# A transformer block whose MLP runs as seven block products: another order of the products, two pairs of them chained in PSUM, half-size load slots, and a rearranged end

## The chip, the core and the metric

The kernel runs on one core of one Trainium2 chip, the other cores being idle. The metric is device microseconds (us) for one execution. The kernel before takes 2223.9 us in the median of three runs (2223.78 to 2226.18).

## The reference, cut to what matters

One block: attention and retention branches, an output projection, a residual, then the MLP. All is float32, 512 tokens, model width 2048, MLP width 8192. The change touches nothing ahead of the MLP's residual, so the rest is shown alone:

```python
    x = x + rms_norm(mix, norm_mix_post[l])
    h = rms_norm(x, norm_mlp_pre[l])
    u = jnp.square(jax.nn.relu(h @ w_up[l]))            # [512, 2048] @ [2048, 8192]
    x = x + rms_norm(u @ w_down[l], norm_mlp_post[l])   # [512, 8192] @ [8192, 2048]
```

## The kernel before, in words

**Seven products.** Each of the two matrix products of the MLP is cut into 2 x 2 parts and computed with seven products P0 to P6 instead of eight, after Strassen and Winograd. Each product multiplies a sum of parts of the activations with a sum of parts of the weights: P0 takes weight part 11, P1 takes 21, P5 takes 22, P2 takes 11+12, P3 takes 12+22, P4 takes 11+12+22 and P6 all four (the tables `ADD` and `SPLIT`). Sums of the products' results give the output: P0+P1 is output part 11, and so on.

**Three matmuls for one.** Float32 is kept by splitting every operand into a high part (fp32r) and the rest: `hi = cast(x)` on ScalarE, `lo = x - hi` on VectorE. `mm3` issues hi by hi, hi by lo and lo by hi into one PSUM tile.

**The up stage** goes through 16 blocks of 2 x 256 columns of w_up; a product is 48 matmuls of 256 columns. **The down stage** goes through 8 chunks of w_down's rows times 2 halves (nb) of its columns, with seven products each; a product is 24 matmuls of 512 columns, and its result is added to one of 14 accumulators in SBUF by VectorE (L1365).

**Order.** A list of phases (block, product) is written out by hand. At its head stand nine early phases, products 0 and 1 of blocks 0 to 3 and product 0 of block 4, which run while the residual, the norm and the sums of the activations (`work3`: `x1_chain`, `x1_out`, `x1_sums`) are still being made. Then come blocks 0, 4, 1, 5, 2, 6, 3, 7, 8 to 15. Blocks 0 to 3 are short there, since two of their products are done.

**The feed.** `Feed` brings the weights: quarters of 1 MB go into slots (`low0`, `low1`, two rows of `Y`, and three lent ones at first) by SyncE's DMA queue (L925). Each product is fed in two slabs of 128 x 1024: where the weight is a sum, VectorE adds it into the slot (L951); ScalarE casts the high part (`whi`, L956); VectorE subtracts (`wlo`, L931) one slab later. The feed stays three slabs ahead of TensorE. For P3 the second summand comes by an accumulating DMA on GpSimd's queue (`late_sum`, L917), but not in blocks 0 to 3. A slot is free again when both its slabs are split.

**Other work.** `up_done` combines the products of a block (VectorE and ScalarE) and stores seven operands of the down stage to DRAM (`keep_u`, L1126, SyncE's queue). `u_operand` loads and splits them for the next chunk (L1288 to L1290). `dn_done` accumulates; in the last chunk it also combines the accumulators (L1370), squares them for the norm (ScalarE, L1310), multiplies by the gain (L1315), takes the roots (L1329, L160, GpSimd L161) and writes the result: rows 0 and 1 of the four token tiles scaled by ScalarE and added into DRAM by accumulating DMAs (`out_first`, L1340, L1341), rows 2 and 3 by VectorE and plain DMAs (`out_last`, L1348, L1349).

Of the kernel before, what the change touches and what calls it, by code (L numbers as in the profile page):

```python
# [10 lines left out]
F32 = mybir.dt.float32  # L11
# [101 lines left out]
def block_kernel(ctx: ExitStack, tc: tile.TileContext, x, norm_mix_pre, w_in, cmp_pe_k, cmp_w1_k, cmp_b1_k,  # L113
# [39 lines left out]
    def mm3(ps, ah, al, bh, bl, first, last):  # L153
        nc.tensor.matmul(ps, ah, bh, start=first, stop=False)  # L154
        nc.tensor.matmul(ps, ah, bl, start=False, stop=False)  # L155
        nc.tensor.matmul(ps, al, bh, start=False, stop=last)  # L156
# [706 lines left out]

    ADD = (None, None, (11, 12), (12, 22), (11, 22), None, (11, 21))
# [20 lines left out]

    class Feed:
# [5 lines left out]
        def __init__(self, phases, slots, ahead, short):  # L892
            self.phases, self.free, self.ahead, self.lent = phases, list(slots), ahead, []
            self.short = short
            self.n, self.at, self.R, self.ready = 0, 0, {}, {}
            self.loads, self.last = [], {}
            for i, (g, prod, source) in enumerate(phases):
                for q in (SPLIT[prod],) if self.by_dma(i) else (ADD[prod] or ()) + (SPLIT[prod],):
                    if (g, q) not in self.last:
                        self.loads.append((g, q, source, i))  # L900
                    self.last[g, q] = i
            self.held = None

        def by_dma(self, i):

            g, prod, _ = self.phases[i]
            return prod == 3 and g not in self.short

        def late_sum(self, i):
# [4 lines left out]
            k = src.shape[1]  # L914
            r = self.R[g, to].rearrange("p (k n) -> p k n", k=k)
            for h in (slice(0, k // 2), slice(k // 2, k)):
                nc.gpsimd.dma_start(r[:, h], src[:, h], accum_op=ALU.add)  # L917

        def load(self, most=99):
            while most and self.loads and self.free and self.loads[0][3] <= self.n // 2 + self.ahead:  # L920
                most -= 1
                g, q, source, _ = self.loads.pop(0)
                r = self.R[g, q] = self.free.pop(0)
                src = source(q)
                nc.sync.dma_start(r.rearrange("p (k n) -> p k n", k=src.shape[1]), src)  # L925

        def low(self):
# [6 lines left out]
            if s:  # L934
                for q in (11, 12, 21, 22):
                    if self.last.get((self.phases[i][0], q)) == i:
                        r = self.R.pop((self.phases[i][0], q))
                        if all(r is not o for o in self.lent):
                            self.free.append(r)

        def advance(self):
# [6 lines left out]
            c = slice(s * SL, (s + 1) * SL)  # L948
            if ADD[prod] and not self.by_dma(i):
                to, by = (self.R[g, q][:, c] for q in ADD[prod])  # L950
                nc.vector.tensor_add(to, to, by)  # L951
            src = self.R[g, SPLIT[prod]][:, c]
# [7 lines left out]
            if prod == 2 and s and (j := [j for j in range(i, min(i + 5, len(self.phases))) if self.by_dma(j)]):  # L960
                self.late_sum(j[0])
# [55 lines left out]
    def x1_out(t):  # L1017
# [16 lines left out]
        for q in range(4):  # L1034
# [5 lines left out]
            nc.vector.tensor_tensor(Y4[:, ks, t, :], pt4, g3T[:, ks, None].to_broadcast([P, 4, P]), op=ALU.mult)  # L1040
# [63 lines left out]
    phases += [(b, p, up_source(b)) for b in blocks for p in ((5, 2, 4, 3, 6) if 0 < b < NPRO else ORDER)  # L1104
# [12 lines left out]
    feed = Feed(phases, [low0, low1], 3, range(NPRO))  # L1117
    tmp = Ring(*xt, *(xh[:, c:c + 512] for c in range(0, 2048, 512)))
    state = [{} for _ in range(NBLK)]

# [4 lines left out]
    def keep_u(k, b, v):  # L1125
        nc.sync.dma_start(ud[k, b], v)  # L1126

    def up_done(b, p, ps):
# [12 lines left out]
        elif p == 1:  # L1141
            z["c11"] = tmp.take()
            nc.vector.tensor_add(v2(z["c11"]), ps, v2(z["p0"]))
            hidden(0, z["c11"])
        elif p == 2:
            if b == 0:
                tmp.views = [Y[:, t, c:c + 512] for t in (1, 3) for c in range(0, 2048, 512)]
            elif b == NPRO:
                tmp.views += xt[:2]
            elif b == NPRO + 1:  # L1150
                tmp.views += xt[2:]
# [336 lines left out]
```

## Time and profile before

| | us |
|---|---|
| median of three runs | 2223.9 |
| the profiled execution | 2220.96 |
| its span, first to last instruction | 2219.2 |
| TensorE busy | 2161.8 (97%) |
| VectorE busy | 1575.4 (71%) |
| ScalarE busy | 994.2 (45%) |
| the MLP's early phases | from about 939 |
| the up stage's full blocks without a gap on TensorE | 1216 to 1570 |
| the down stage up to the last chunk | about 1575 to 2110 |
| the last matmul ends | about 2200.7 |

TensorE is busy nearly all the time, so what it does not do in the remaining 57 us, and how long it is given half its clock, is where time can be found. Busy time is read with care: a matmul's record is longer than the step from one matmul to the next, so a stretch is best measured by how many matmuls it holds.

### The profile page before, as it was taken

What the parts mean: (1) busy time and instruction counts of PE and PEld (TensorE: products, weight loads), DVE (VectorE), ACT (ScalarE), POOL (GpSimd) and SP (SyncE); (2) the same over time, 40 slices, a digit from 0 to 9 for tenths busy, and PEclk for the clock granted to TensorE, in tenths of its full rate; (3) what the DMA queues carried; (4) which work ended last, traced back from release to release, by engine and by line L of the source; (5) the groups of instructions that cost most, each with busy time, mean ns of one, the idle gap of its engine ahead of it and who ended that gap; (6) DMA issues with size and microseconds to landing.
All of it is one profiled execution on the core that took longest, in us unless ns stands there. A gap on an engine that the chain in (4) does not pass through costs nothing.

```text
span 2219.2 us, 31801 instructions
## 1 busy us (share of the span) xinstructions
PE 2161.8 (97%) x12787; PEld 1915.4 (86%) x12787; DVE 1575.4 (71%) x1880; ACT 994.2 (45%) x1440; POOL 111.1 (5%) x131
## 2 busy tenths in 40 slices
PE   8999999999999999989999999999999999999995
PEld 7888878878778899989999999999888888888874
DVE  6213555554556533598888878878879999999998
ACT  5213343343332323575555555555664454445443
POOL 0000000000000000000000000000000000000001
PEclk9999999999999999999999999999999999999998
DMA  6543324323224334565655766767675656566664
GB/s 192 136 122 88 93 65 95 95 72 91 81 72 138 98 103 142 186 221 171 207 172 169 225 179 183 190 174 209 223 229 161 216 163 218 160 197 175 192 187 86
DMA packets 248054, 342.67 MB, mean 154 GB/s; under 512 B 14011, under 2 KB 159755, under 8 KB 247009
## 3 DMA queue, kind: packets, MB, share of 16 engines
q1 hardware_dynamic: 213440, 292.43, 40.6%
q0 software_dynamic: 24368, 36.67, 10.3%
q10 hardware_dynamic: 10098, 11.55, 1.5%
q8 instruction: 100, 1.64, 0.3%
q14 instruction: 48, 0.39, 0.1%
HBM read 298.85 MB, written 41.75 MB: 153 GB/s over the span
## 4 chain that ended last, share of the span: by engine, by line
PE 87%; DVE 8%; ACT 2%; issue 1%; DMA 1%; POOL 0%; SPq 0%; DVEq 0%; POOLq 0%; ACTq 0%
PE prod L156 16%; PE prod L155 16%; PE prod L154 16%; PE mm L154 11%; PE mm L156 11%; PE mm L155 11%; DVE wlo L931 2%; PE S L583 2%; PE S L706 1%; PE PT L646 1%; PE oT L741 1%; PE oT L501 1%; PE oT L154 1%; DVE Y L951 1%; DMA low<-in_w_up 1%
## 5 line engine op out<-in xcount | busy, mean ns | idle before, releaser
L956 ACT CAST whi<-low 128x1024 fp32r<-128x1024 f32 x230 | 242.1, 1053 | 277.5 <-PE prod L156 134.9
L155 PE MATMUL prod<-wlo,Hh 128*128 128x512 f32 x896 | 350.5, 391 | 11.5 <-DVE wlo L931 11.4
L956 ACT CAST whi<-Y 128x1024 fp32r<-128x1024 f32 x212 | 222.6, 1050 | 285.7 <-PE prod L156 119.9
L144 DVE TENSOR_TENSOR wlo<-raw,whi 128x1024 fp32r<-128x1024 f32 (+4 forms) x152 | 168.6, 1113 | 255.4 <-ACT whi L143 250.6
L156 PE MATMUL prod<-whi,Hl 128*128 128x512 f32 x896 | 349.4, 390 | 0.0
L154 PE MATMUL prod<-whi,Hh 128*128 128x512 f32 x896 | 349.3, 390 | 0.0
L931 DVE TENSOR_TENSOR wlo<-low,whi 128x1024 fp32r<-128x1024 f32 x230 | 280.1, 1221 | 48.2 <-ACT whi L956 47.3
L156 PE MATMUL prod<-Hh,wlo 128*128 128x256 f32 x1024 | 285.3, 279 | 13.4 <-DVE wlo L931 13.4
L931 DVE TENSOR_TENSOR wlo<-Y,whi 128x1024 fp32r<-128x1024 f32 x212 | 258.4, 1221 | 38.7 <-ACT whi L956 37.7
L154 PE MATMUL prod<-Hh,whi 128*128 128x256 f32 x1024 | 284.7, 278 | 0.3 <-ACT Hh L143 0.3
L155 PE MATMUL prod<-Hl,whi 128*128 128x256 f32 x1024 | 284.0, 277 | 0.9 <-DVE Hl L144 0.9
L143 ACT CAST whi<-raw 128x1024 fp32r<-128x1024 f32 (+4 forms) x152 | 145.6, 960 | 302.2 <-PE mm L155 148.0
L154 PE MATMUL mm<-whi,Hh 128*128 128x416 f32 (+4 forms) x704 | 263.1, 374 | 0.5 <-ACT Hh L143 0.5
L156 PE MATMUL mm<-whi,Hl 128*128 128x416 f32 (+4 forms) x704 | 248.6, 353 | 0.5 <-DVE Hl L144 0.5
L155 PE MATMUL mm<-wlo,Hh 128*128 128x416 f32 (+4 forms) x704 | 248.1, 352 | 0.0
L156 PE MATMUL prod<-sx,wlo 128*128 128x256 f32 x768 | 212.3, 276 | 2.6 <-DVE wlo L931 2.6
L154 PE MATMUL mm<-Hh,whi 128*128 128x512 f32 x512 | 214.7, 419 | 0.1
L154 PE MATMUL prod<-sx,whi 128*128 128x256 f32 x768 | 212.0, 276 | 0.0
L155 PE MATMUL prod<-sx,whi 128*128 128x256 f32 x768 | 212.0, 276 | 0.0
L155 PEld LDWEIGHTS prod<-wlo,Hh 128*128 128x128 f32 x896 | 168.7, 188 | 49.7 <-DVE wlo L931 14.8
L156 PEld LDWEIGHTS prod<-Hh,wlo 128*128 128x128 f32 x1024 | 192.9, 188 | 15.3 <-DVE wlo L931 15.2
L156 PE MATMUL mm<-Hh,wlo 128*128 128x512 f32 x512 | 200.5, 392 | 0.0
(265 smaller groups left out, 3969.9 us busy)
## 6 DMA issues: line engine op xcount, KB each, us to landing
raw<-in_w_in SPq DMA_DIRECT2D x160, 256.0 KB, 3.1
low<-in_w_up SPq DMA_DIRECT2D x38, 1024.0 KB, 6.0
Y<-in_w_up SPq DMA_DIRECT2D x32, 1024.0 KB, 6.3
Y<-in_w_down SPq DMA_DIRECT2D x32, 1024.0 KB, 5.2
low<-in_w_down SPq DMA_DIRECT2D x32, 1024.0 KB, 5.2
Y<-ud SPq DMA_DIRECT2D x49, 512.0 KB, 9.0
ud<-Y SPq DMA_DIRECT2D x77, 256.0 KB, 4.3
raw<-in_w_out SPq DMA_DIRECT2D x32, 416.0 KB, 3.5
```

Of the source, the lines that this page charges most:

```text
L143: nc.scalar.copy(hi, src)
L144: nc.vector.tensor_sub(lo, src, hi.bitcast(F32))
L154: nc.tensor.matmul(ps, ah, bh, start=first, stop=False)
L155: nc.tensor.matmul(ps, ah, bl, start=False, stop=False)
L156: nc.tensor.matmul(ps, al, bh, start=False, stop=last)
L501: nc.tensor.matmul(hid[:65, :DK], kv[:, l:l + STRIDE * 64 + 1:STRIDE], w1s[l // 16][:, l % 16, :], start=l == 0, stop=l == CBLK - 1)
L583: nc.tensor.matmul(sps[:, :c + L], QT[g][:, h, qs], k, start=True, stop=True)
L646: nc.tensor.transpose(pt[:, e * P:(e + 1) * P], Pt[:, e, rows_of(j)], ident)
L706: nc.tensor.matmul(sps[:, :n], QK[:, 2 + d, rows_of(j)], QK[:, d, j * P:], start=d == 0, stop=d == 1)
L741: nc.tensor.matmul(o[:, :DR], AT[:, a0:a0 + P], vr[:, j, :], start=j == 0, stop=j == i)
L931: nc.vector.tensor_sub(lo, src, hi.bitcast(F32))
L956: nc.scalar.copy(hi, src)
```

## The change

- **Order of the products.** A full block and every down group run 0 2 1 4 3 5 6 (before 0 1 2 5 4 3 6). Blocks 0 to 4 run 1 2 5 4 3 6 less what the early phases did. The early phases go through two blocks together: P0 of both, then P1 of both.
- **Chains in PSUM.** P1 accumulates onto P0's PSUM tile, with P2 between them; in the down groups and from block 5 on, P6 accumulates onto P3's, with P5 between. A class `Banks` hands out the three PSUM tile pairs. P0 and P3 are still read out when they are done.
- **Sums in `up_done`** are rearranged to fit: P0+P1 comes out of PSUM through ScalarE's Relu (before: an add on VectorE, then Relu), P3 is subtracted straight from PSUM.
- **Half slots.** Loads, slots and releases are by halves of 512 KB, in the order in which slabs need them; there are six lent halves.
- **P3's second summand by DMA everywhere**, and in the last chunk P6's as well (`tight`).
- **`keep_u`** issues from ScalarE's queue (before SyncE's).
- **x1_out**: for token tiles 2 and 3 half of the gains are applied by ScalarE, four instructions of 128 x 128, in place of one of VectorE.
- **The last chunk**: accumulators of one row lie side by side, so that the output is scaled and written 1024 columns at a time; the roots of rows 0 and 1 stay after the last P5, but scaling and writing these rows move behind the last product's first half.

```diff
-        def __init__(self, phases, slots, ahead, short):
+        def __init__(self, phases, slots, ahead, tight):
+            self.phases, self.free, self.ahead, self.lent = phases, [h for r in slots for h in halved(r)], ahead, []
...
-            return prod == 3 and g not in self.short
+            return prod == 3 or prod == 6 and g in self.tight
...
-            if s:
-                for q in (11, 12, 21, 22):
-                    if self.last.get((self.phases[i][0], q)) == i:
-                        r = self.R.pop((self.phases[i][0], q))
+            for q in (11, 12, 21, 22):
+                if self.last.get((self.phases[i][0], q)) == i:
+                    r = self.R.pop((self.phases[i][0], q, s))
...
+            if t >= 2 and q % 2:
+                for j in range(4):
+                    k = 4 * q + j
+                    nc.scalar.activation(Y4[:, k, t, :], pt4[:, j, :], AF.Copy, scale=g3T[:, k:k + 1])
+            else:
+                nc.vector.tensor_tensor(Y4[:, ks, t, :], pt4, g3T[:, ks, None].to_broadcast([P, 4, P]), op=ALU.mult)
...
-    ORDER = (0, 1, 2, 5, 4, 3, 6)
-    early = [(b, p) for b in range(NPRO) for p in (0, 1)] + [(NPRO, 0)]
+    ORDER = (0, 2, 1, 4, 3, 5, 6)
+    early = [(b + n, p) for b in range(0, NPRO, 2) for p in (0, 1) for n in (0, 1)] + [(NPRO, 0)]
...
+    class Banks:
+
+
+        def __init__(self):
+            self.free, self.held = [pr0], {}
+
+        def chained(self, g, p):
+
+            b = g if isinstance(g, int) else g[0]
+            return p in (0, 1) and b != NPRO or p in (3, 6) and (b == "down" or b > NPRO)
+
+        def take(self, g, p):
+
+            group = g if not isinstance(g, int) and g[0] == "down" else g if isinstance(g, int) else g[0]
+            if self.chained(g, p) and p in (1, 6):
+                self.now = self.held.pop((group, p))
+                self.free.append(self.now[0])
+                return self.now[1], True
+            pool = self.free.pop(0)
+            ps = pool.tile([P, 2, S], F32, name="prod")
+            if self.chained(g, p):
+                self.held[group, {0: 1, 3: 6}[p]] = pool, ps
+            else:
+                self.free.append(pool)
+            return ps, False
...
     def keep_u(k, b, v):
-        nc.sync.dma_start(ud[k, b], v)
+        nc.scalar.dma_start(ud[k, b], v)
...
+                nc.scalar.activation(v2(z["c11"]), ps, AF.Relu)
+                later.add(1, lambda: nc.scalar.activation(z["c11"], z["c11"], AF.Square))
+                later.add(3, lambda: keep_u(0, b, z["c11"]))
...
+            z["c22"] = tmp.take()
+            nc.vector.tensor_sub(v2(z["c22"]), v2(z["v"]), ps)
+            hidden(6, z["c22"])
...
+        else:
+            lasts = []
+            for t in (0, 1):
+                add(e[6][:, t], ps[:, t], e[6][:, t])
+                square(1, 21, 2 + t, e[6][:, t])
+                gained(1, 21, e[6], slice(t, t + 1))
+                for parts in lasts:
+                    next(parts)
+                root(2 + t)
+                out_first(t)
+                lasts.append(out_last(2 + t))
+                next(lasts[-1])
+            next(lasts[-1])
```

What this does to VectorE at the beginning of short block 1, before, from P2's second `wlo` on (`low` and `Y` are weight slots; a row on 128x1024 with two slots is a weight sum, the 128x512 rows combine products):

```order
L1184 TENSOR_TENSOR Y_5587<-Y_5587 128x512
L951 TENSOR_TENSOR Y_5587<-Y_5587,low1_7097 128x1024
L931 TENSOR_TENSOR wlo_8862<-Y_5587,whi_8861 128x1024
L951 TENSOR_TENSOR Y_5587<-Y_5587,low1_7097 128x1024
L931 TENSOR_TENSOR wlo_8897<-Y_5587,whi_8896 128x1024
L951 TENSOR_TENSOR low0_7099<-low0_7099,low1_7097 128x1024
L931 TENSOR_TENSOR wlo_8931<-Y_5587,whi_8930 128x1024
L951 TENSOR_TENSOR low0_7099<-low0_7099,low1_7097 128x1024
L931 TENSOR_TENSOR wlo_8961<-low0_7099,whi_8960 128x1024
```

and now, from P5's second `wlo` on, through P4 and P3 to P6's first sum:

```order
L1232 TENSOR_TENSOR Y_5587<-Y_5587 128x512
L956 TENSOR_TENSOR Y_5587<-Y_5587 128x1024
L938 TENSOR_TENSOR wlo_8894<-Y_5587,whi_8893 128x1024
L956 TENSOR_TENSOR Y_5587<-Y_5587 128x1024
L938 TENSOR_TENSOR wlo_8928<-Y_5587,whi_8927 128x1024
L938 TENSOR_TENSOR wlo_8962<-Y_5587,whi_8961 128x1024
L938 TENSOR_TENSOR wlo_8992<-low1_7097,whi_8991 128x1024
L956 TENSOR_TENSOR Y_5587<-Y_5587,low0_7099 128x1024
```

P3's two weight sums have left VectorE, and P4's stand between products that need none.

VectorE's last rows before the final product, before (`acc` and `xh` are accumulators, `xrow` the gain; the last two `wlo` feed the final product):

```order
L1370 TENSOR_TENSOR acc9_14666<-acc9_14666,acc7_14664 128x1024
L951 TENSOR_TENSOR low0_7099<-low0_7099,low1_7097 128x1024
L931 TENSOR_TENSOR wlo_18788<-Y_5587,whi_18787 128x1024
L1365 TENSOR_TENSOR acc11_14668<-prod_18764,acc11_14668 128x1024
L1370 TENSOR_TENSOR xh_7103<-xh_7103,acc9_14666 128x1024
L1370 TENSOR_TENSOR xh_7103<-xh_7103,acc7_14664 128x1024
L1315 TENSOR_TENSOR acc8_14665<-acc8_14665,xrow_7098 128x1024
L1389 TENSOR_TENSOR xh_7103<-xh_7103,acc11_14668 128x1024
L1370 TENSOR_TENSOR acc9_14666<-acc9_14666,acc11_14668 128x1024
L951 TENSOR_TENSOR low0_7099<-low0_7099,low1_7097 128x1024
L931 TENSOR_TENSOR wlo_18807<-low0_7099,whi_18806 128x1024
L931 TENSOR_TENSOR wlo_18834<-low0_7099,whi_18833 128x1024
```

and now (`two` and `xh` hold two accumulators each):

```order
L1431 TENSOR_TENSOR acc10_14679<-prod_18769,acc10_14679 128x1024
L1419 TENSOR_TENSOR two2_14675<-two2_14675,acc10_14679 128x1024
L938 TENSOR_TENSOR wlo_18812<-low1_7097,whi_18811 128x1024
L1419 TENSOR_TENSOR xh_7103<-xh_7103,two2_14675 128x1024
L938 TENSOR_TENSOR wlo_18830<-Y_5587,whi_18829 128x1024
L1419 TENSOR_TENSOR two2_14675<-two2_14675,acc13_14680 128x1024
L1439 TENSOR_TENSOR two2_14675<-two2_14675,prod_18810 128x1024
L1419 TENSOR_TENSOR two2_14675<-two2_14675,acc10_14679 128x1024
L938 TENSOR_TENSOR wlo_18848<-Y_5587,whi_18847 128x1024
L938 TENSOR_TENSOR wlo_18871<-Y_5587,whi_18870 128x1024
```

The two weight sums of the final product are gone from here. From the read-out of the last chunk's first P0 to the last `wlo`, both included, VectorE had 69 rows and has 59.

GpSimd's last rows before (`st` 5588 to 5591 are the statistics of rows 0 to 3, the DMAs add rows 0 and 1 into the output):

```order
L161 TENSOR_TENSOR st_5588<-st_5588,misc 128x1
L161 TENSOR_TENSOR st_5589<-st_5589,misc 128x1
L1341 DMA out<-acc_14658 128x512
L1341 DMA out<-acc_14662 128x512
L1341 DMA out<-acc_14665 128x512
L1341 DMA out<-xh 128x512
L1341 DMA out<-acc_14658 128x512
L1341 DMA out<-acc_14662 128x512
L1341 DMA out<-acc_14665 128x512
L1341 DMA out<-xh 128x512
L161 TENSOR_TENSOR st_5590<-st_5590,misc 128x1
L161 TENSOR_TENSOR st_5591<-st_5591,misc 128x1
```

and now:

```order
L162 TENSOR_TENSOR st_5588<-st_5588,misc 128x1
L162 TENSOR_TENSOR st_5589<-st_5589,misc 128x1
L162 TENSOR_TENSOR st_5590<-st_5590,misc 128x1
L1393 DMA out<-two_14673 128x2x512
L1393 DMA out<-xh 128x2x512
L162 TENSOR_TENSOR st_5591<-st_5591,misc 128x1
L1393 DMA out<-two_14673 128x2x512
L1393 DMA out<-xh 128x2x512
```

The accumulating output DMAs now stand behind the roots of rows 2 and 3.

## Rows read from the trace of the kernel before

**Rows 1.** The page's busy time: us, share of the span, instructions.
```profile
PE 2161.8 (97%) x12787; PEld 1915.4 (86%) x12787; DVE 1575.4 (71%) x1880; ACT 994.2 (45%) x1440; POOL 111.1 (5%) x131
```
**Rows 2.** Windows: stretch, length, busy us (instructions) of PE PEld DVE ACT POOL, PEclk, DMA.
```profile
939.00:1000.00 61.00, 55.08 (x460) 54.30 (x460) 54.70 (x63) 41.88 (x56) 2.68 (x3) 0.97 0.69 229
1000.00:1216.00 216.00, 205.69 (x1788) 204.01 (x1787) 180.13 (x183) 112.75 (x139) 7.68 (x6) 1.00 0.61 183
1216.00:1570.00 354.00, 354.00 (x3120) 354.00 (x3119) 290.12 (x292) 197.76 (x242) 22.92 (x18) 1.00 0.68 190
1600.00:2100.00 500.00, 500.00 (x2207) 414.17 (x2206) 450.81 (x390) 245.25 (x240) 30.75 (x26) 1.00 0.62 187
2100.00:2200.80 100.80, 89.69 (x377) 71.41 (x376) 100.00 (x92) 46.94 (x66) 9.16 (x12) 0.97 0.46 133
```
**Rows 3.** PE's waits in 939:1000, 1000:1216, 2090:2220: us in total, times, longest.
```profile
PE prod L156 <- DVE wlo L931: 5.8, 4, 3.8
...
PE prod L156 <- DVE wlo L931: 10.3, 8, 1.9
...
PE prod L155 <- DVE wlo L931: 11.0, 6, 6.0
```
**Rows 4.** Timeline of DVE in short block 1: start, us, instruction [idle before <-releaser].
```profile
1064.52 1.23 DVE L951 TENSOR_TENSOR Y<-Y,low 128x1024 f32<-128x1024 f32 x1 [2.55 <-DMA low<-in_w_up]
...
1072.32 1.22 DVE L951 TENSOR_TENSOR Y<-Y,low 128x1024 f32<-128x1024 f32 x1
1073.46 1.22 DVE L931 TENSOR_TENSOR wlo<-Y,whi 128x1024 fp32r<-128x1024 f32 x1
```
**Rows 5.** Timeline of ACT, then of DVE, near the end of the early phases.
```profile
977.81 1.05 ACT L956 CAST whi<-low 128x1024 fp32r<-128x1024 f32 x1 [2.36 <-DMA low<-in_w_up]
...
981.45 1.23 DVE L144 TENSOR_TENSOR Hl<-Y,Hh 128x1024 fp32r<-128x1024 f32 x1 [1.71 <-ACT Hh L143]
...
995.08 1.21 DVE L931 TENSOR_TENSOR wlo<-low,whi 128x1024 fp32r<-128x1024 f32 x1
```
**Rows 6.** DVE's groups in 1216:1570 by shape: count, busy us, mean ns.
```profile
L931 DVE TENSOR_TENSOR wlo<-low,whi 128x1024 fp32r<-128x1024 f32 x68 | 82.7, 1223 | 20.8 <-ACT whi L956 20.4
...
L1163 DVE TENSOR_TENSOR Y<-Y 128x512 f32<-128x512 f32 x7 | 4.8, 692 | 0.2
```
**Rows 7.** DVE's timeline in the last chunk: first P0 read out; last two `wlo`.
```profile
2114.99 1.22 DVE L1365 TENSOR_TENSOR acc<-prod,acc 128x1024 f32<-128x1024 f32 x1
...
2191.78 2.47 DVE L931 TENSOR_TENSOR wlo<-low,whi 128x1024 fp32r<-128x1024 f32 x2
```
**Rows 8.** Timeline of the end.
```profile
2197.42 2.69 POOL L1341 DMA_DIRECT2D out<-acc  x3 [0.53 <-ACT acc L1340]
...
2203.96 0.68 DVE L1359 TENSOR_TENSOR xh<-prod,xh 128x512 f32<-128x512 f32 x1
...
2207.18 1.41 DVE L1348 SCALAR_TENSOR_TENSOR acc<-acc,st,Y 128x512 f32<-128x512 f32 x2 [0.74 <-POOL st L161]
...
2215.81 0.33 SPq L1349 DMA_DIRECT2D out<-acc  x1
```
**Rows 9.** Windows of one us at the end (columns of rows 2; last: DMA share, GB/s).
```profile
2195.00:2196.00 1.00, 1.00 (x4) 0.81 (x3) 0.93 (x6) 0.00 (x0) 0.19 (x1) 0.50 0.00 0
...
2208.00:2209.00 1.00, 0.00 (x0) 0.00 (x0) 1.00 (x2) 0.00 (x0) 0.00 (x0) 0.50 1.13 205
...
2216.00:2217.00 1.00, 0.00 (x0) 0.00 (x0) 0.00 (x0) 0.00 (x0) 0.00 (x0) 0.50 1.05 369
```
**Rows 10.** DMA issues over the span: KB each, median us to landing.
```profile
low<-in_w_up SPq DMA_DIRECT2D x38, 1024.0 KB, 6.0
...
raw<-in_w_in SPq DMA_DIRECT2D x24, 512.0 KB, 4.6
```
**Rows 11.** L1126, the stores of `keep_u`: duration of an issue, ns, min/median/max.
```profile
L1126 SPq DMA_DIRECT2D ud<-Y x77: 319/338/2945, 1023.8 to 1581.9; - x77
```
**Rows 12.** L1349, the plain output writes: from issue to landing.
```profile
DMA to landing us min/median/max: 2.3/2.5/5.1
```

More of the change, by code (lines that the diff above doesn't have):

```diff
@@ L151, in wide, with mm3 @@
         return bass.AP(tensor=g.tensor, offset=g.offset + c0, ap=[[0, P], [1, n]])
[L153 to L156, printed above, removed]
+    def mm3(ps, ah, al, bh, bl, first, last, more=False):
+        nc.tensor.matmul(ps, ah, bh, start=first, stop=False, skip_group_check=more)
+        nc.tensor.matmul(ps, ah, bl, start=False, stop=False, skip_group_check=more)
+        nc.tensor.matmul(ps, al, bh, start=False, stop=last, skip_group_check=more)
     def inv_root(dst, ss, tmp, n, scale):
@@ L1189, in block_kernel, with up @@
     sets = []
-    def up(n0, n1, pools, xa):
+    def up(n0, n1, xa):
         for i in range(n0, n1):
@@ L1195, in up @@
             b = g if isinstance(g, int) else g[0]
-            ps = pools[i % len(pools)].tile([P, 2, S], F32, name="prod")
+            ps, more = banks.take(g, p)
             for s in range(2):
@@ L1207, in up @@
                         mm3(ps[:, f, :256], hi[:, kk, rows_of(f)], lo[:, kk, rows_of(f)], xh[:, k, :], xl[:, k, :],
-                            k == 0, k == 7)
+                            k == 0 and not more, k == 7, more)
                     yield
@@ L1217, in primed @@
         yield
-    feed.load(1)
+    feed.load(2)
     for q in range(4):
         x_fetch(0, q)
-    feed.load(1)
+    feed.load(2)
+    feed.ahead = -NPRO
     outs = [x1_out(t) for t in range(NT)]
@@ L1236, in block_kernel @@
     prp = prctx.enter_context(tc.tile_pool(name="prim", bufs=1, reuse_waits="tile"))
-    feed.lent = [prp.tile([P, 2048], F32, name=f"pre{i}") for i in range(3)]
+    feed.lent = [prp.tile([P, SL], F32, name=f"pre{i}") for i in range(6)]
     feed.free = feed.lent + feed.free
@@ L1277, in block_kernel @@
     last = nup - 4
-    for _ in up(len(early), last, pools, XA):
+    for _ in up(len(early), last, XA):
         pass
@@ L1323, in squares @@
                 square(nb, q, q // 10 * 2 - 2 + t, v[:, t])
-            vec.append(lambda: gained(nb, q, v, slice(0, 2)))
-        act.append(squares)
+            later.add(1, lambda: slow.append(lambda: gained(nb, q, v, slice(0, 2))))
+        later.add(1, squares)
     def root(t):
@@ new lines, in dn_done @@
+            add(e[2], ps, e[2])
+        elif p == 1:
+            add(e[1], ps, e[1])
+            there(nb, 11, e[1])
+        elif p == 4:
+            flush(vec)
+            add(e[0], ps, e[0])
+            op(sub, 2, 0)
+            op(add, 5, 2)
+            op(sub, 2, 3)
+            op(add, 6, 0)
+        elif p == 3:
+            while len(vec) > 1:
+                vec.pop(0)()
+            sub(e[2], e[2], ps)
+            there(nb, 22, e[2])
+        elif p == 5:
+            flush(vec)
+            add(e[5], ps, e[5])
+            if not nb:
+                there(nb, 12, e[5])
+                return
+            for t in (0, 1):
+                square(nb, 12, t, e[5][:, t])
+            flush(slow)
+            gained(nb, 12, e[5], slice(0, 2))
+            root(0)
+            root(1)
+        elif not nb:
+            add(e[6], ps, e[6])
+            there(nb, 21, e[6])
+        else:
+            lasts = []
+            for t in (0, 1):
+                add(e[6][:, t], ps[:, t], e[6][:, t])
[8 more added lines that the diff above has]
+            next(lasts[-1])
@@ L1418, in block_kernel @@
     sets2 = []
     def down():
-        for i, ((_, c, nb), p, _) in enumerate(phases[nup:]):
-            ps = pools[(nup + i) % len(pools)].tile([P, 2, S], F32, name="prod")
+        for i, (g, p, _) in enumerate(phases[nup:]):
+            _, c, nb = g
+            ps, more = banks.take(g, p)
             final = nup + i == len(phases) - 1
@@ L1426, in down @@
             for s in range(2):
-                slabs.append([v.rearrange("p (k n) -> p k n", k=2) for v in feed.slab()])
+                while len(slabs) <= (1 if final else s):
+                    slabs.append([v.rearrange("p (k n) -> p k n", k=2) for v in feed.slab()])
                 if s == 0 and sets2:
@@ L1449, in down @@
                             mm3(ps[:, t, :], uh[:, k, rows_of(t)], ul[:, k, rows_of(t)], slabs[s2][0][:, kk, :],
-                                slabs[s2][1][:, kk, :], k == 0, k == 3)
+                                slabs[s2][1][:, kk, :], k == 0 and not more, k == 3, more)
             sets2.append((c, nb, p, ps))
         dn_done(*sets2.pop())
-    for n, _ in enumerate(up(last, nup, pools, XA)):
+    for n, _ in enumerate(up(last, nup, XA)):
         if n % 4 == 2 and n < 16:
```

191 lines of the change are left out of this document (82 added, 109 removed).

## The prediction

> **What bounds the kernel now.** I read the page's busy line first [rows 1]: TensorE is busy 97% of the span, and the change keeps every matmul. So it can give back only time in which TensorE waits or is slow, and I looked for that by windows of the span, counting matmuls [rows 2]. In 1216:1570 nothing waits: 3120 matmuls of 256 columns in 354 us, 0.1135 us each, so an up product of 48 takes 5.45. In 1600:2100 the 2207 matmuls of 512 columns take 0.2266 each, a down product of 24 takes 5.44. Against these steps the other stretches lose: 939:1000 has 460 matmuls, 52.2 us, and lasts 61: 8.8 lost, some of it transposes and start-up. 1000:1216 has 1788, 202.9 us, and lasts 216: 13.1 lost. 2100:2200.8 has 377, 85.4 us, and lasts 100.8: 15.4 lost. After that 18.4 us pass without a matmul. The list of waits names one cause in all three stretches: TensorE waits for `wlo`, the subtraction on VectorE [rows 3]. The listed waits (5.8, 10.3, 11.0) are smaller than the losses, because a record is longer than a step and hides the first part of each wait, and because after a long wait TensorE gets the lower of its two clock levels (granted 0.50, that is 1.2 instead of 2.4 GHz) for some matmuls [rows 9].
>
> So each stretch is a question of VectorE's queue. A row of 128x1024 stands at 1.22 us, one of 128x512 at 0.69 [rows 6].
>
> **Term 1, early phases (8.8 us lost).** The last wait, 3.8 us, ends with the `wlo` at 995.08 [rows 3, 5]. Going back from it VectorE is full to 981.45, where it waited 1.71 for a cast of the last normalised tokens; from that row to the `wlo`, both included, stand 13 rows, and the changed order has the same 13. The change takes four adds (P1 of blocks 0 to 3) and four gain rows off VectorE, 8 x 0.69 = 5.5 us, but nearly all ahead of that cast. There VectorE waits for TensorE's last transposes by way of ScalarE, which now applies the gain in four instructions. I therefore expect little: the 2.36 us that ScalarE waits for a weight at 977.81 [rows 5] go, since half slots are freed earlier, and the cast comes perhaps 1 us sooner. Gain 2. Bounds: nothing, if the transposes alone set it; 6 us, the 5.5 taken off VectorE and half a microsecond of clock, if the freed rows count in full.
>
> **Term 2, short blocks (13.1 us lost).** In block 1 VectorE idles 2.55 us at 1064.52, its row's weight not landed; TensorE then waits twice, the second time behind P2's and P4's weight sums at 1072.32 and 1073.46 [rows 4]. Two things made it late. First the slot: a weight for P2 takes a slot that is freed three slabs before it is needed, three slabs being 8.2 us, of which the split itself takes about one slab, and a load of 1024 KB lands in 6.0 [rows 10]. In the new order I count four to six slabs between freeing and need, for halves. The nearest row for a load of 512 KB is 4.6 us [rows 10]. That is 2.7 us or more of extra time and 1.4 of shorter landing, against a wait of 2.55.
>
> Second VectorE's load: a short block has 10 `wlo` and 8 weight sums, 18 x 1.22, and 10 rows of 0.69, 28.9 us, while TensorE needs 5 x 5.45 = 27.2. Without P3's two sums it is 26.4, and P4's sums stand between products without any (the first order in the part on the change). Both causes go together. Gain 11.5 of 13.1. Bounds: 6, if VectorE at 97% still comes late in each short block; 13.1.
>
> **Term 3, last chunk.** VectorE is busy 100.0 of 100.8 us [rows 2], so its rows are the clock. The first P0 is read out at 2114.99; the last `wlo` starts one row after 2191.78, at 2193.0, and ends at 2194.25 [rows 7]. Between the two starts are 68 steps in 78.0 us, 1.147 each. The new order has 58 steps: 66.5 us, so the last `wlo` starts at 2181.5 and ends at 2182.7. TensorE without waits would want the final product's slabs at 2115.0 + 12 x 5.44 = 2180.3 and 1.4 later; it now waits some 1 us in all, too little to cost the clock, and its last matmul comes near 2187 instead of 2200.7. The feed's end is what counts, 11.5 us earlier. If VectorE idles here and there, as it can now that it is hardly overfull, up to 3 us of that are lost.
>
> What follows the last `wlo` lasted 2219.2 - 2194.25 = 25 us before. Now stand on VectorE: two large rows, a wait for ScalarE's two squares, a large row and the four short rows of the roots, about five large rows' time or 5.6 us; the first half's chain from its add to its scaled write, 2207.18 - 2203.96 = 3.2 [rows 8]; two halves of 0.7; the second half's chain, 3.2 with two halves of 0.7 inside it; three halves more. The last write is issued near 17.3, and from the last issue to the span's end were 3.4 us (2215.81 to 2219.2), so by VectorE the end is at 20.7.
>
> The output DMAs are a second limit. While accumulating ones run, the DMA engines are full (1.13) at 205 GB/s; while plain ones run, at 369 [rows 9]. 2 MB of each are 10.2 + 5.7 = 15.9 us at least. Before, they started at 2197.42 [rows 8], 3.2 after the last `wlo`. Now they stand behind the root of row 2 (third order in the part on the change), 5.6 + 3.2 after it, with first data one issue later, at 10. If the two kinds share the engines they end at 10 + 15.9 = 25.9, and 26.8 with the 0.9 that the program's end takes; if the plain writes of SyncE's queue pass beside the others, at 20.7. A plain write took 2.5 us in the median and up to 5.1 [rows 12], the long ones beside accumulating ones, which speaks for sharing. I take 25, as long as before, which is near the full engines; the bounds are 20.7 and 28.
>
> *The Trainium skill on this.* The Trainium skill, "DMA: Bandwidth & Descriptors", section "Issuing engines are not separate DMA queues", says that whatever engine issues a DMA, it runs on the same 16 DMA engines and interleaves there, so that a second queue saves only issue time. By that rule the end is at 26.8 and the term 9.7 instead of 11.5; by the opposite it would be 15.8. Rows 9 and 12 agree with the rule, which speaks against moving the accumulating writes behind the last product.
>
> Gain of the term: 11.5. Bounds: 11.5 + 4.3 = 15.8, and 11.5 - 3 - 3 = 5.5.
>
> **What costs nothing.** The chains: P1 and P6 wait until P0 and P3 have been read out of the same PSUM tile, but one product (5.4 us) stands between, and VectorE's read-out stands ahead of the `wlo` that TensorE needs anyway; if it lagged, the same `wlo` would. Down groups still read seven times, so 1600:2100, where TensorE is already full, keeps its time. In 1216:1570 VectorE loses two rows of 0.69 per block, beside a full TensorE: nothing. ScalarE's 112 stores: an issue took 338 ns in the median on SyncE [rows 11], four in a row 1.4 us, and ScalarE has 354 - 197.8 = 156 us idle over 65 products [rows 2], 2.4 each. For small new waits at places that I don't see I take 1 us off.
>
> **Sum.** 2 + 11.5 + 11.5 - 1 = 24. The profiled execution's span of 2219.2 becomes 2195.2, its time of 2220.96 about 2197; the median of the three runs lies 2.9 above that, so 2223.9 - 24 = 2199.9, say 2200.
>
> **Rivals.**
> *A, the end gives it back.* The output DMAs start late on full engines and the idle of VectorE shows: term 3 is 3 to 5.5, the sum 16 to 18: 2206 to 2208. For it: rows 9 show the engines full. Against it: the first half of the work now starts to be written with fewer and larger DMAs, and the feed ends 11 us sooner whatever follows.
> *B, the short blocks stay late.* P6 of a full block and P2 of a short one put eight rows of 1.22 and some of 0.69 into two products, 11 us of 10.9. If that makes each of the four wait 2 us, term 2 is 3 to 5, the sum 16 to 18, and the time 2206 to 2208. For it: VectorE at 97%. Against it: the two slabs before need no sum.
> *C, ScalarE is held by its stores (slower).* A store issued from ScalarE holds the casts behind it while it waits for VectorE's results or for an older transfer. The longest issue on SyncE was 2.945 us [rows 11]; there only loads stood behind. If two of the four stores of a block are held so long, that is 6.6 us, 4.2 over ScalarE's idle, by 16 blocks 67: 2200 + 67 = 2267. It decides, that is the change is lost, from 1.5 us of wait per block. Against it: the results are finished a slab before the stores, and each store waits for a transfer some ten issues back.
> *D, the early phases open.* Term 1 gives 6: 2196, inside the forecast's range.
>
> **How the numbers follow.** Forecast with D 0.78 (2189 to 2205), A 0.10, B 0.08, C 0.04. The range of 2189 to 2211 leaves out C and some of the edges. A change of 0.2%, 4.4 us, is about what a measurement tells from none. All but C lie more than that below 2223.9, and a mixture of A, B and a mild C may end near it: faster 0.94, same 0.02, slower 0.04.
>
> **What would show it.** Right: no listed wait of TensorE for `wlo` above 1 us between 1030 and 1216, the down chunks starting 12 to 14 us earlier, at most 2 us of waits in the last chunk with the clock staying at its upper level until the last matmul, and about 25 us from the last `wlo` to the end. The wait of some 4 us before the first full block still there. Wrong: ScalarE idle on DMA or VectorE in the up stage with TensorE waiting behind it; a gap in 1216:1570; more than 28 us after the last `wlo`.

## The result, and the profile after

The changed kernel takes 2202.0 us in the median of four runs (2200.95 to 2203.66), against 2223.8 for the kernel before in the same comparison: the ratio is 0.9904, 95% interval 0.9886 to 0.9921. The forecast was 2200. In the profiled executions the span went from 2219.2 to 2199.0, 20.2 us less where 24 were forecast. The page's busy line and the windows, with the columns of [rows 1, 2]:

```profile
PE 2154.7 (98%) x12787; PEld 1910.5 (87%) x12787; DVE 1535.1 (70%) x1828; ACT 984.4 (45%) x1425; POOL 122.7 (6%) x139
```

```profile
939.00:1000.00 61.00, 55.86 (x471) 55.12 (x470) 50.90 (x53) 47.47 (x74) 3.94 (x5) 0.97 0.75 240
1000.00:1216.00 216.00, 216.00 (x1903) 216.00 (x1903) 182.54 (x185) 116.24 (x139) 15.57 (x13) 1.00 0.77 215
...
1600.00:2100.00 500.00, 500.00 (x2208) 414.01 (x2207) 455.84 (x394) 244.49 (x240) 31.68 (x27) 1.00 0.64 191
```

In 1000:1216 now stand 1903 matmuls where 1788 stood, and TensorE is busy all the time. The waits of TensorE in 939:1000 and in 2090:2200 (us, times, longest; 1000:1216 lists none any more), against [rows 3]:

```profile
PE prod L157 <- DVE wlo L938: 5.1, 3, 3.8
...
PE prod L156 <- DVE wlo L938: 2.1, 4, 1.2
```

VectorE in the last chunk, against [rows 7]: the first P0 is read out, ScalarE's squares are waited for (three such rows), and the last `wlo` starts.

```profile
2099.77 1.21 DVE L1422 TENSOR_TENSOR acc<-prod,acc 128x1024 f32<-128x1024 f32 x1
...
2115.13 1.23 DVE L1366 TENSOR_TENSOR two<-two,xrow 128x1024 f32<-128x1024 f32 x1 [0.42 <-ACT jk L1361]
...
2168.48 1.23 DVE L938 TENSOR_TENSOR wlo<-Y,whi 128x1024 fp32r<-128x1024 f32 x1 [0.21 <-ACT whi L961]
```

The 58 steps between the first and the last of these rows take 68.7 us (before: 68 steps in 78.0). The last `wlo` ends at 2169.7, 24.5 us sooner, and TensorE's last matmul at 2173.9. In its last us the granted clock (third number from the end) is still 1.00, the upper level, where the last product began at 0.50 before [rows 9]:

```profile
2173.00:2174.00 1.00, 0.91 (x5) 0.41 (x3) 0.42 (x1) 0.55 (x2) 0.00 (x0) 1.00 0.00 0
```

From the last `wlo` to the end are 29.3 us, though, where 25 were before. The timeline of the end, against [rows 8]: first read-out, the accumulating writes of rows 0 and 1, VectorE's last rows.

```profile
2175.23 0.68 DVE L1459 TENSOR_TENSOR two<-prod,two 128x512 f32<-128x512 f32 x1
...
2178.38 1.22 POOL L1393 DMA_DIRECT2D out<-two  x1
...
2184.19 2.61 DVE L1403 SCALAR_TENSOR_TENSOR two<-two,st,Y 128x1024 f32<-128x1024 f32 x3 [0.75 <-POOL st L162]
2184.86 1.66 POOL L1393 DMA_DIRECT2D out<-xh  x1
```

The DMA view of 2176 to 2199, in 40 slices of 0.575 us (busy tenths, GB/s), and its queues (packets, MB, share of the 16 engines' time there; q0 holds the accumulating writes, q1 the plain ones):

```profile
DMA  0000000959999999999999999999999999982000
GB/s 0 0 0 0 0 0 0 64 64 178 203 214 214 370 413 210 221 214 221 253 328 371 278 239 249 271 260 264 267 257 260 249 271 249 274 285 82 4 0 0
...
q0 software_dynamic: 1088, 2.10, 52.9%
q1 hardware_dynamic: 1120, 2.10, 26.2%
```

VectorE is done at 2186.8. The DMA engines are busy nearly without a gap from 2180.0 to 2196.7, and the span ends 2.3 us later. The accumulated 2.1 MB cost them twice the time of the plain 2.1 MB.

Gains in the two profiled executions, by the start of the products and the `wlo` rows:

| part | forecast | measured |
|---|---|---|
| first 50 us of the program, which the change does not touch | 0 | 1.3 |
| early phases (term 1) | 2 | 1.0 |
| short blocks (term 2) | 11.5 | 12.9 |
| down chunks before the last | 0 | 0.7 |
| last chunk, start to last `wlo` (term 3) | 11.5 | 8.6 |
| last `wlo` to the end (term 3) | 0 | -4.3 |
| unseen waits | -1 | 0 |
| sum | 24 | 20.2 |

### The profile page after: what moved, and what is told of

The parts are those of the page before. It is cut to its first block, busy times and chain, and to the rows that moved or that the text cites. A ratio compares the mean times of both kernels' runs of the same rounds, so it can differ in the third digit from the quotient of the medians.

```text
span 2199.0 us, 31984 instructions
## 1 busy us (share of the span) xinstructions
PE 2154.7 (98%) x12787; PEld 1910.5 (87%) x12787; DVE 1535.1 (70%) x1828; ACT 984.4 (45%) x1425; POOL 122.7 (6%) x139
## 4 chain that ended last, share of the span: by engine, by line
PE 90%; DVE 5%; issue 1%; ACT 1%; DMA 1%; POOL 0%; SPq 0%; DVEq 0%; ACTq 0%; POOLq 0%
PE prod L157 17%; PE prod L155 17%; PE prod L156 17%; PE mm L155 11%; PE mm L157 11%; PE mm L156 11%; PE S L584 2%; DVE wlo L938 2%; PE PT L647 1%; PE S L707 1%; PE oT L742 1%; PE oT L502 1%; PE oT L155 1%; PE oT L156 1%; PE oT L157 1%
## 5 line engine op out<-in xcount | busy, mean ns | idle before, releaser
L961 ACT CAST whi<-Y 128x1024 fp32r<-128x1024 f32 x227 | 238.2, 1050 | 283.1 <-PE prod L157 117.6
L961 ACT CAST whi<-low 128x1024 fp32r<-128x1024 f32 x215 | 226.4, 1054 | 265.1 <-PE prod L157 131.6
L938 DVE TENSOR_TENSOR wlo<-Y,whi 128x1024 fp32r<-128x1024 f32 x227 | 276.8, 1220 | 51.5 <-ACT whi L961 50.5
L938 DVE TENSOR_TENSOR wlo<-low,whi 128x1024 fp32r<-128x1024 f32 x215 | 262.1, 1221 | 55.9 <-ACT whi L961 55.0
L156 PE MATMUL mm<-Hl,whi 128*128 128x512 f32 x512 | 200.0, 391 | 0.0
```

Source lines behind the costliest of these rows:

```text
L156: nc.tensor.matmul(ps, ah, bl, start=False, stop=False, skip_group_check=more)
L938: nc.vector.tensor_sub(lo, src, hi.bitcast(F32))
L961: nc.scalar.copy(hi, src)
```

## The experiments

"The changed kernel" is at 2202.0. Each kernel was timed beside the kernel before; times are medians of four or more runs, and the intervals of the ratios are some 0.0015 to each side, 3.5 us. A stretch is therefore also read from the trace. The tail, last `wlo` to the end, is free of what the start of the program does by chance, but not of all chance: in the changed kernel and the six variants that leave its end alone (4 to 9) it lies between 28.7 and 30.7 us.

**1. Both rows' accumulating writes early.**

```diff
                 root(2 + t)
-                out_first(t)
+                if not t:
+                    out_first(0)
+                    out_first(1)
```

> The changed kernel with one thing moved: both token rows 0 and 1 are scaled and their accumulating writes issued behind the root of row 2, so that the second pair is issued about 2180.5 and 2181.6 instead of 2184.1 and 2184.9. Theory F (the DMA engines are full from 2180 to 2197 in the changed kernel, so the amount of transfer decides and not when it is issued): the engines carry the same bytes in the same 16.7 us, the end moves by less than 1 us, 2201 to 2203. Theory S (the late second pair sets the end): the end comes by the 3.5 us earlier, 2198 to 2199.

Measured 2202.9, ratio 0.9908 (0.9891 to 0.9924); the tail is 29.6 us. GpSimd's timeline:

```profile
2180.33 1.22 POOL L1393 DMA_DIRECT2D out<-two  x1
2181.09 1.69 POOL L1393 DMA_DIRECT2D out<-xh  x1
2182.09 1.91 POOL L1393 DMA_DIRECT2D out<-two  x1
2183.13 2.10 POOL L1393 DMA_DIRECT2D out<-xh  x1
```

The second pair follows the first by 2 us instead of 5.7, and the end does not come earlier: 29.6 is inside the tail's scatter. Theory F holds, S falls.

**2. No accumulating writes.**

```diff
             nc.scalar.activation(v, v, AF.Copy, scale=st[t][:, 7:8])
-            nc.gpsimd.dma_start(wide2(out[rows_of(t), nb * 1024:(nb + 1) * 1024]), v, accum_op=ALU.add)
```

> The changed kernel without the four accumulating output writes; rows 0 and 1 of the result are left as the residual (part of the computation is left out). It prices these writes. Theory F: only 2 MB of plain writes remain, 5.7 us at 369 GB/s, which fit beside VectorE's chain; the last write is issued near 2187.3 as VectorE's last row ends at 2186.8, and 3.4 us later the span ends, 2190.7 against 2199.0: 8 us less, about 2194. Theory V (VectorE's chain and the program's end set it, the writes are hidden anyway): at most 3 us less, 2199 or more.

Measured 2194.7, 7.4 less, and a tail of 21.2 us. From the last `wlo` to the end the accumulating writes cost 8.1 us. Without them VectorE's chain, the other bound, sets the end at 21.2 (the forecast had 20.7 for it). The DMA view of 2176 to 2200 shows plain writes with idle time between:

```profile
DMA  0000000000003990079500899970000000000000
```

**3. Rows 0 and 1 written plainly.**

```diff
+                    r = x1a[t, nb] = feed.free.pop(0)
+                    nc.sync.dma_start(r, out[rows_of(t), nb * 1024:(nb + 1) * 1024])
...
-            nc.scalar.activation(v, v, AF.Copy, scale=st[t][:, 7:8])
-            nc.gpsimd.dma_start(wide2(out[rows_of(t), nb * 1024:(nb + 1) * 1024]), v, accum_op=ALU.add)
+            nc.vector.scalar_tensor_tensor(v, v, st[t][:, 7:8], x1a[t, nb].rearrange("p (j n) -> p j n", n=S),
+                                           op0=ALU.mult, op1=ALU.add)
+            nc.sync.dma_start(wide2(out[rows_of(t), nb * 1024:(nb + 1) * 1024]), v)
```

> The changed kernel with rows 0 and 1 also written plainly: the residual of these rows is read back into four weight slots that the last chunk no longer needs (2 MB, while the DMA engines are half idle), VectorE scales and adds (four more rows of 128x1024, 1.28 us each) and SyncE writes. The roots of rows 0 and 1 go ahead of a gain, and both halves of the final product are read out ahead of the scaling. Theory F: 4 MB plain at 369 GB/s are 11.4 us from about 2179, so the last bytes land at 2191 and the span ends near 2192.5, 6.5 us less than 2199.0: about 2195.5. Theory V: VectorE gets 5.1 us more, its last row ends near 2188.5 instead of 2186.8, and the end is not earlier than now less the time that the moved roots save (1 us): 2201 or more.

Measured 2196.8, ratio 0.9877 (0.9862 to 0.9891), tail 23.6 us, 5.7 less: theory F, although VectorE has more to do. The moved roots and read-outs, 1 us by the expectation's estimate, are part of this and were not tried alone. The DMA view of 2176 to 2200:

```profile
DMA  0000000099301999999999999999900000000000
GB/s 0 0 0 0 0 0 0 0 352 386 137 0 72 386 372 382 372 386 362 379 386 379 396 369 382 375 386 386 345 3 0 0 0 0 0 0 0 0 0 0
...
q1 hardware_dynamic: 2208, 4.19, 47.0%
```

All 4.2 MB now go at some 380 GB/s and take 47.0% of these 24 us, 11 us of engine time.

**4. P6's sums of the last chunk back on VectorE.**

```diff
-    feed = Feed(phases, [low0, low1], 3, [("down", NCH - 1, nb) for nb in range(2)])
+    feed = Feed(phases, [low0, low1], 3, [])
```

> The changed kernel with the sums of the final chunk's P6 weights back on VectorE (four rows of 128x1024, two for each half of the columns) in place of the accumulating DMAs. Theory D (VectorE's rows are the clock of the last chunk, 1.147 us each): four steps cost 4.6, less the 1.5 us that VectorE waits there now: 3 to 4.6 us slower, 2205 to 2206.6. Theory T (TensorE's own steps and the waits for ScalarE's squares bind the last chunk of the changed kernel, VectorE has slack): up to 1.5 us slower, 2202 to 2203.5.

Measured 2206.6, 4.6 slower; first read-out and last `wlo`:

```profile
2100.61 1.22 DVE L1422 TENSOR_TENSOR acc<-prod,acc 128x1024 f32<-128x1024 f32 x1
...
2173.69 1.23 DVE L938 TENSOR_TENSOR wlo<-low,whi 128x1024 fp32r<-128x1024 f32 x1
```

That is 73.1 us against 68.7: 4.4 for four rows. TensorE's listed waits grow from 2.1 to 5.9. Theory D: VectorE's rows are still the clock of the last chunk.

Experiments 5 to 7 undo one edit each that bears on the short blocks, 8 the move of the stores.

**5. P3's sums on VectorE in blocks 0 to 3.**

```diff
-            return prod == 3 or prod == 6 and g in self.tight
+            return prod == 3 and g not in range(4) or prod == 6 and g in self.tight
```

> The changed kernel with P3's two weight sums back on VectorE in blocks 0 to 3. Theory L (VectorE's load made the short blocks late): a short block is again 20 rows of 1.22 and some of 0.69, 28.9 us against TensorE's 27.2, so up to 1.7 us per block come back: 4 to 7 us slower than the changed kernel, 2206 to 2209, with waits of TensorE for the low part between 1030 and 1216. Theory S (the slots and the landing of the loads did it, and half slots mend that): at most 1 us slower, 2201 to 2203.

**6. Slots released as a whole.**

```diff
-                    r = self.R.pop((self.phases[i][0], q, s))
-                    if all(r is not o for o in self.lent):
-                        self.free.append(r)
+                    for h in range(2) if s else ():
+                        r = self.R.pop((self.phases[i][0], q, h))
+                        if all(r is not o for o in self.lent):
+                            self.free.append(r)
```

> The changed kernel with slots freed only when both halves are split; loads still go by halves. Theory S: the first half of a weight comes one slab (2.7 us) later than now, waits of VectorE or ScalarE for a load like the 2.55 us of before come back in the short blocks, and TensorE waits for the low part there: 4 to 11 us slower than the changed kernel, 2206 to 2213. Theory L: the loads are early enough with the new order, at most 1 us slower.

**7. P5 ahead of P2 in blocks 1 to 3.**

```diff
-    phases += [(b, p, up_source(b)) for b in blocks for p in ((1, 2, 5, 4, 3, 6) if b <= NPRO else ORDER)
+    phases += [(b, p, up_source(b)) for b in blocks for p in ((1, 5, 2, 4, 3, 6) if 0 < b < NPRO else (1, 2, 5, 4, 3, 6) if b <= NPRO else ORDER)
```

> The changed kernel with blocks 1 to 3 in the order 5 2 4 3 6 of before (now 2 5 4 3 6), half slots and P3's sums by DMA kept. P2's and P4's four weight sums then stand in successive products again. Theory O (the spacing of the sums counts): two products hold 8 rows of 1.22 and the combining rows of 0.69, over 11 us against 10.9, and TensorE waits up to 2 us in each of three blocks: 3 to 6 us slower, 2205 to 2208. Rival (half slots and two sums less give slack enough): at most 1 us slower.

**8. The stores on SyncE.**

```diff
-        nc.scalar.dma_start(ud[k, b], v)
+        nc.sync.dma_start(ud[k, b], v)
```

> The changed kernel with the stores of the down stage's operands issued by SyncE again. The forecast put their move at nothing, since ScalarE has 2.4 us idle in each product: within 1 us of the changed kernel, 2201 to 2203. Rival C' (ScalarE's issues delay its casts): the changed kernel gets faster by 2 us or more without them. Rival Q (on SyncE a store holds the loads behind it): 2 us slower or more, with waits for a load in the up stage.

Measured for 5 to 8: 2203.8, 2203.9, 2202.4 and 2202.6. None differs from the changed kernel by more than the measurement tells. With the sums on VectorE and with P5 first, TensorE has no listed wait in 1000:1216, so theories L and O fall as they stood. With whole release ScalarE waits once in the short blocks for a load, and TensorE's product there takes 7.3 us instead of 5.4:

```profile
1072.40 1.05 ACT L962 CAST whi<-Y 128x1024 fp32r<-128x1024 f32 x1 [5.00 <-DMA low<-in_w_up]
```

So release by halves matters once, 1.9 us and not the 4 to 11 that theory S gave it. The stores make no difference that can be told on either queue. Either the three edits stand in for each other, or something else did it; the next three runs ask that.

**9. All three undone.** The diffs of 5, 6 and 7 together, in the changed kernel.

> The changed kernel with the three edits undone together that made hardly a difference one by one: P3's sums on VectorE in blocks 0 to 3, slots freed as a whole, P5 ahead of P2 in blocks 1 to 3. Theory R (each of the three alone leaves VectorE enough slack, so that either of the others covers for the one undone): the waits of the short blocks come back, 8 to 13 us slower than the changed kernel, 2210 to 2215. Rival N (something else in the change took them away, the chains in PSUM, the combining rows or the stores): at most 4 us slower, 2202 to 2206.

Measured 2203.6, ratio 0.9904 (0.9891 to 0.9918), and no listed wait of TensorE in 1000:1216. Theory R falls. The loads still go by halves here, in the order in which slabs need them; that is left as a possible cause, beside parts of the change that have nothing to do with these three.

**10. The kernel before with P3's sums by DMA.**

```diff
-            return prod == 3 and g not in self.short
+            return prod == 3
```

> The kernel before with one edit: P3's second summand by an accumulating DMA in blocks 0 to 3 too. Theory R: the two rows less per block and a slot that is freed earlier are enough alone, 8 to 13 us faster than before, 2211 to 2216. Rival S (a whole slot and a load of 1024 KB still come late at the head of each short block): at most 4 us faster, 2219 to 2224.

Measured 2223.2 against 2224.2, ratio 0.9993 (0.9984 to 1.0001): no change that can be told, as rival S has it. VectorE still waits for loads. TensorE's waits in 1000:1216, and VectorE's for loads in 1030:1216:

```profile
PE prod L156 <- DVE wlo L931: 9.4, 8, 1.9
```

```profile
DVE Y L951 <- DMA low<-in_w_up: 5.3, 2, 2.7
...
DVE Y L951 <- DMA Y<-in_w_up: 2.7, 1, 2.7
```

**11. The kernel before with half slots.** The whole of `Feed` as in the change (loads, slots and releases by halves), order and sums as before.

```diff
-        feed.free += [Y[:, 0, :], Y[:, 2, :]]
+        feed.free += halved(Y[:, 0, :]) + halved(Y[:, 2, :])
...
-    feed.lent = [prp.tile([P, 2048], F32, name=f"pre{i}") for i in range(3)]
+    feed.lent = [prp.tile([P, SL], F32, name=f"pre{i}") for i in range(6)]
```

> The kernel before with one edit: loads, slots and releases by halves. Theory R: loads in time are enough alone, 8 to 13 us faster than before, 2211 to 2216. Rival L (VectorE's 28.9 us of rows in 27.2 keep it late): at most 4 us faster, 2219 to 2224.

Measured 2211.0 against 2224.2, ratio 0.9940 (0.9926 to 0.9953): theory R for the loads holds, rival L falls. TensorE's waits in 1000:1216; VectorE waits for no load there any more:

```profile
PE prod L156 <- DVE wlo L936: 1.4, 3, 0.5
```

From the first product of block 0 to the end of block 7 stand 40 products, 218.0 us at 5.45 each. In the trace this stretch lasts 221.4 us here, 231.3 in the kernel before and 218.4 in the changed one, so half slots alone are worth 10 of the 12.9. Of the 3 us that are left, 2.2 are the three waits, one in P2's second half in each of blocks 1 to 3. In block 1 VectorE has four rows that combine products (the fourth is shown) and then the weight sum ahead of the `wlo` that TensorE waits for:

```profile
1066.62 0.69 DVE L1189 TENSOR_TENSOR Y<-Y 128x512 f32<-128x512 f32 x1
1067.23 1.22 DVE L954 TENSOR_TENSOR low<-low,Y 128x1024 f32<-128x1024 f32 x1
1068.36 1.22 DVE L936 TENSOR_TENSOR wlo<-Y,whi 128x1024 fp32r<-128x1024 f32 x1
```

The other 1 us stands in the first five products, which take 5.65 without a listed wait; no run explains it.

**12. Plain rows, the end packed.** The kernel of experiment 3 with its end rearranged:

```diff
+            nc.vector.tensor_tensor(spared, e[5], g4[:, None, cols(nb, 1)].to_broadcast([P, 2, S]), op=ALU.mult)
...
+            root(0)
+            root(1)
+            for t in (0, 1):
+                add(e[6][:, t], ps[:, t], e[6][:, t])
+                square(1, 21, 2 + t, e[6][:, t])
+            first = [out_first(t) for t in (0, 1)]
+            next(first[0])
+            next(first[1])
+            gained(1, 21, e[6], slice(0, 2))
```

> The kernel with rows 0 and 1 written plainly, its end packed more densely: the last gain of the P5 row goes into a spare slot while VectorE waits for TensorE's last matmul, the roots of rows 0 and 1 ahead of the final read-outs, and the first column halves of both rows ahead of the second gain. VectorE's last row then ends near 2189 instead of 2190.2 and the first write is issued some 1.3 us earlier, so by theory F (4 MB at 380 GB/s from the first write on) the end comes 1 us sooner: about 2195.8. Rival: VectorE and the engines end together now and nothing is left there: 2196 to 2198.

Measured 2194.7, ratio 0.9864 (0.9851 to 0.9878), tail 21.9 us, 1.7 less than in experiment 3 where 1 was expected. This version is ahead of both kernels, by 29.4 us of the one before and, medians against medians, by 7.3 of the changed one. VectorE's timeline at the end of TensorE's work: the gain fills the wait that stood here (1.98 us in experiment 3), and the first scaled row is done 1.5 us sooner.

```profile
2173.92 1.23 DVE L1469 TENSOR_TENSOR low<-xh,xrow 128x1024 f32<-128x1024 f32 x1
...
2177.09 1.28 DVE L1409 SCALAR_TENSOR_TENSOR two<-two,st,low 128x1024 f32<-128x1024 f32 x1
```

## Why the prediction came out as it did

**What bounds the kernel: right.** Up to the last matmul, and apart from the 1.3 us at the program's start, what was gained is time in which TensorE waited or ran at its lower clock; its matmuls keep their steps (2208 in 1600:2100 as 2207 before). Most signs came as named: no listed wait in the short blocks, 3.8 us before the first full block, the upper clock until the last matmul, 2.1 us of waits in the last chunk. The down chunks start 15.2 us earlier, 13.9 without the program's start. The tail passed its sign of being wrong, 28 us.

**Term 1: about 1 us, forecast 2.** From the first early product to the first of block 0 the changed kernel loses 12.5 us against nine products of 5.45, the kernel before 13.5. The kernels with the change's early part lose between 12.5 and 14.1 over eleven profiles (mean 13.0), the three with that of before between 13.5 and 14.4 (mean 13.8), so that 1 us is near the scatter. The reason given, that the last transposes and ScalarE's gains set the beginning of the chain, is what the trace shows. VectorE is less busy, but it waits 2.41 us there for the cast, and from that row to the `wlo` stand the same 13 rows; the wait of 3.8 us stayed, as forecast.

```profile
979.31 1.23 DVE L144 TENSOR_TENSOR Hl<-Y,Hh 128x1024 fp32r<-128x1024 f32 x1 [2.41 <-ACT Hh L143]
...
992.94 1.22 DVE L938 TENSOR_TENSOR wlo<-low,whi 128x1024 fp32r<-128x1024 f32 x1
```

**Term 2: 12.9 us, forecast 11.5, the bound of 13.1 nearly reached.** The first cause, a load that comes late, was right and is most of it: half slots alone take 10 us, and the waits for loads are gone. The second cause, VectorE's 28.9 us of rows for 27.2 of matmuls, was wrong as a cause of its own. Taking two rows per block off the old kernel gave nothing measurable (experiment 10), and putting them back cost nothing that shows (5, 9). A likely reason, which no run tries by itself: rows that exceed TensorE's time by 1.7 us in one short block can be made up in the full block next to it, where VectorE has slack (290 us busy of 354 in 1216:1570 [rows 2]). Rival B rested on the same argument and fell with it. What takes the last 3 us is not isolated: it is none of the three edits of 5 to 7 alone or together, since experiment 9 is without waits. The rearranged combining rows are a candidate, since the waits left in experiment 11 end behind such rows; they were not tried alone. Halves can help in two ways, by earlier slots and by loads that land earlier and in the order of need. Whole release made TensorE wait once behind a late load in experiment 6 and not at all in 9, so the second seems to weigh more. On the kernel before the two were not taken apart.

**Term 3, feed: 8.6 to 9.3 us, forecast 11.5.** The count of 58 steps was right, and experiment 4 shows that a row still costs its 1.1 us. The steps took 1.185 us on average instead of 1.147, 2.2 us in all, mostly since VectorE waited four times (1.5 us) for ScalarE, a squaring ahead of a gain in three of them. The forecast had allowed up to 3 us for that.

**Term 3, tail: the step that failed.** The forecast took 25 us between 20.7, by VectorE's chain, and 26.8, by full DMA engines; it is 29.3, above even the bound of 28. Experiment 2 measures 21.2 for the chain, and the engines got their first data 10.3 us after the last `wlo` (forecast 10) and were full for 16.7 (15.9). The step that failed is the choice of a value between the two limits, as if VectorE's chain could still shorten what full engines that start late set alone; that is 1.8 of the 4.3 us. The other 2.5 are in the larger limit itself: first data 0.3 later, 0.8 more of full engines, and 2.3 instead of 0.9 from there to the end. The rule cited from the Trainium skill, "DMA: Bandwidth & Descriptors", section "Issuing engines are not separate DMA queues", that DMAs from all issuing engines interleave on the same 16 DMA engines, agrees with this trace: both queues together fill the engines from 2180.0 to 2196.7. Experiment 1 shows that issuing the second pair earlier did not move the end; no run issued the same writes from another queue. Experiments 2 and 3 show what moves it, the amount of engine time.

**Rivals.** A's mechanism came true: term 3 gave 4.3, inside A's 3 to 5.5. Its time of 2206 to 2208 was not reached, since four things that the forecast had otherwise brought 4.4 us: term 2 1.4, the unneeded allowance for unseen waits 1.0, the down chunks 0.7, and the start of the program, where nothing was changed, 1.3. Term 1 took 1.0 of that back. That the total lies near 2200 is thus partly luck: errors that cancel. C did not come: the stores' issues on ScalarE last 383 ns in the median, the longest 1202, and on either queue the time is the same as far as can be told (experiment 8).

```profile
L1166 ACTq DMA_DIRECT2D ud<-Y x77: 326/383/1202, 1023.0 to 1570.2; - x77
```

D did not come either: term 1 gave 1.0 and not 6.

## What to carry to other kernels

When a sum of two loaded pieces comes late, cut the loads to what the first step needs and order them by step before taking work off the engine that waits; an engine that is overfull in one short block but has slack in the next is not yet a bound. When two limits of a tail are worked out, take at least the larger one, not a value between them, and price the transfers in engine time: what was accumulated in DRAM cost twice here. Work that reads its operand back early, while the DMA engines have time, and writes plainly can be the better end even if the busiest engine gets more rows.

## What the runs showed of the hardware

- Accumulating and plain writes of 2.1 MB each took 52.9% and 26.2% of the DMA engines' time in the same 23 us, a ratio of 2.0. Mixed they moved some 260 GB/s, plain ones alone some 380 (experiment 3). The accumulating writes come from GpSimd's queue and the plain ones from SyncE's, and experiment 3 changes both at once. A plain load on GpSimd's queue speaks against the queue as the cause: in 49:54 of the changed kernel its 0.52 MB take 31.7% of 5 us, 3.0 us per MB, where the plain writes take 2.9 and the accumulating ones 5.8. It is a load and not a write, so the two are not quite taken apart.

```profile
q0 software_dynamic: 144, 0.52, 31.7%
```

- Beside accumulating writes on full engines a plain write landed after 6.5 to 10.5 us, where 2.3 to 5.1 were seen before [rows 12], and an issue on SyncE lasted up to 1.5 us. With plain writes alone on engines just as full, the last six of experiment 3 landed after 3.4 to 4.0. L1405 in the changed kernel (issue in ns, min/median/max; landing), then the landing of experiment 3's last six:

```profile
L1405 SPq DMA_DIRECT2D out<-two x6: 356/762/1512, 2179.7 to 2187.4; - x6
...
DMA to landing us min/median/max: 6.5/9.0/10.5
...
DMA to landing us min/median/max: 3.4/3.8/4.0
```

- The first 50 us of the program, alike in all these kernels, differ by up to 2.7 us between the fourteen profiled executions, more than term 1 is worth; the first early product starts between 936.5 and 939.6.
